# A hybrid RWKV-7 and DeltaNet block: lanes that take turns every 1280 dense columns, later norm sums, and a TensorE queue in emission order

## The chip, the cores and the metric

The kernel runs on one core of one Trainium2 chip. The metric is device time in microseconds (us). TensorE is PE in the views (its weight loads PEld), VectorE is DVE, ScalarE is ACT, GpSimd is POOL, and SP is the queue that issues nearly all transfers.

## The reference, cut to what matters

One layer over 256 latent and 256 context tokens of width 2048, in float32. An adaLN-modulated norm feeds one wide projection. Its columns go to an RWKV-7 branch (16 heads of 64, handled as 8 pairs), a gated DeltaNet branch (8 heads of 128) and merge gates:

```python
p = h @ in_w
pa, pb, pg = split_cols(p, [A_COLS, B_COLS, GATE_COLS])
ya, ya_c = rwkv7_branch(...)      # token shift, then two scans (forward and reverse) over the tokens
yb, yb_c = gdn_branch(...)        # conv, silu, l2 norm, then chunked scans
x = x + g1 * ((gate_a * (ya @ up_a) + gate_b * (yb @ up_b)) @ out_w)
x = x + g2 * squared_relu_mlp(modulate(rms_norm(x, norm2_w), sh2, sc2), mlp_w1, mlp_w2)
```

In the RWKV scan, `S_t = S diag(w) - (S kk) b^T + v k^T`; the kernel does it in chunks of 64 tokens, with the inverse of a triangular matrix per chunk. DeltaNet does likewise in chunks of 128.

## The kernel before, in words

Every large product is dense: weights are read in granules of 512 KB, split into a rounded part `hi` on ScalarE (L226) and a rest `lo` on VectorE (L227), and `mm3` (L239 to L241) issues three matmuls for each 128 rows of the contraction (a k-step), on 256 columns (latent tokens alone) or 512 (both). Results gather in two banks of PSUM (`dacc`, pool `psd`).

The middle of the kernel is the weave (L180). One generator, `dense`, goes through the projections of the layer and yields after each k-step with its cost, columns over 800. Beside it stand three lanes: `chains` (the recurrences: eight RWKV chains, then eight DeltaNet chains), `invs` (the triangular inversions) and `preps` (what an inversion and a chain need). After each dense yield, a lane whose due time has come emits one step or more; a step's cost is its yield times the lane's factor. A lane waits (`until`) for sets such as `ready`, `prepped`, `begun`, `done` and `read`, which are filled as the other generators are emitted; while `dense` itself is in an `until`, it yields 0.5 without a matmul.

A chain step is a group of small matmuls (L878, L896, L912 with L917 and L919) and the evictions of its result, on ScalarE or VectorE (L175 in the views, where a helper records them); the next step reads what was evicted. An inversion (`tri_inv`, L469) is 62 small operations on VectorE between transposes, after which L818, L828 and L841 use it on TensorE (L1153 on for DeltaNet). `prep2` emits L676, L678, L751, L748, L778 and L789 for each pair of heads. A norm sum (L611 for q and k, L654 for the RWKV key) is one matmul on squares that several evictions made. `gemv_steps` (L279) multiplies the modulation's weights (L296), one step per so many dense yields (`every`, MR).

The order of emission isn't the order of the queues. The tool that lays the queues out gives each engine the earliest emitted instruction that it takes to be ready, so a ready instruction can overtake one that isn't; `high_priority` (V1, S1, G1 and the casts) moves instructions ahead. SP's queue is laid out in the same way.

Of the kernel before, what the change touches and what calls it, by code (L numbers as in the profile page):

```python
# [20 lines left out]
NP = 8  # L21
# [5 lines left out]
CW, F_C, F_P, Q, GW, F_GP, GCW, F_GC, NG, MR, Y = 1.5, 1.5, 0.9, 0.0, 1.65, 0.9, 1.2, 0.6, 2, 16, (2, 2.5, 2, 2, 0, 1)  # L27
# [104 lines left out]
def body(tc, A, out, dbg=None):  # L132
# [146 lines left out]
    def gemv_steps(n, pool, acc, ahead=0):  # L279
# [3 lines left out]
        for q in range(4):  # L283
            raws = []
            for i in range(2):
                raw = pool.tile([128, 1024], F32, tag="raw", name="raw", bufs=ahead) if ahead else \
                    stream.tile([128, 1024], F32, tag="graw", name="graw", bufs=2)
                r0 = (4 * q + 2 * i) * 128
                nc.sync.dma_start(out=raw.rearrange("p (k c) -> p k c", k=2),
                                  in_=A["mod_w"][r0:r0 + 256, n * 512:(n + 1) * 512].rearrange("(k p) c -> p k c", p=128))  # L290
                raws.append(raw)
            if not ahead:
                yield
            for g in range(4):
                k = 4 * q + g
                P.matmul(out=pm[32 * g:32 * g + 32, :], lhsT=sc_st[:, 2 * k:2 * k + 32], rhs=raws[g // 2][:, g % 2 * 512:g % 2 * 512 + 512],  # L296
                         start=(q == 0), stop=(q == 3), skip_group_check=True)
            if q < 3:
                yield
        rows = (pool() if callable(pool) else pool).tile([128, 512], F32, tag="pt", name="rows", bufs=2)  # L300
        S.copy(out=rows, in_=pm)
        return rows, pm
# [103 lines left out]
    def projg(src, ncol, xonly):  # L406
# [3 lines left out]
        for g in range(2):  # L410
            wg = wgran(src[:, 8 * g:8 * g + 8, :])
            for kk in range(8):
                k = 8 * g + kk
                mm3(ps[:ncol, :n], *wk_(wg, kk, ncol), hT[k][0][:, tsl], hT[k][1][:, tsl], k == 0, k == KT - 1)
                yield n / 800
# [75 lines left out]
    def gate(j, tile_):  # L491

        ps = yield from projg(A["w_pg"][j], 128, True)
# [29 lines left out]
    with ExitStack() as st:  # L523
# [12 lines left out]
        def decays():  # L536
# [31 lines left out]
            V.tensor_scalar(out=bb, in0=bb, scalar1=0.5, scalar2=0.5, op0=ALU.mult, op1=ALU.add)  # L568
            for d in range(2):
# [12 lines left out]
                V.tensor_tensor(out=nbk, in0=nbk, in1=nb, op=ALU.mult)  # L582
                P.transpose(q[0:32, 128:256], gc, ident)
# [25 lines left out]
        def l2n(dst, n, bias, q, sq):  # L609
            S.activation(out=sq[:, :n], in_=dst[:, :n], func=AF.Square)  # L610
# [6 lines left out]
            V.tensor_tensor(out=dst[:, :n], in0=dst[:, :n], in1=sq[:, :n], op=ALU.mult)  # L617

        def gproj(h):
            ps = yield from projg(A["w_gdn"][h], 128, True)  # L620
            qv = ptile("qv")
            l2n(qv, 256, C("lnq"), ps, conv_silu(ps, qv, h, 256))
            nc.sync.dma_start(out=spq[h], in_=qv[:, :256])
            ps = yield from projg(A["w_gdn"][8 + h], 128, False)
            kv = ptile("kv")
            l2n(kv, 512, None, ps, conv_silu(ps, kv, 8 + h, 512))
            nc.sync.dma_start(out=spk[h], in_=kv)
            ps = yield from projg(A["w_gdn"][16 + h], 128, False)
# [9 lines left out]
        def prep(p, R):  # L638
# [6 lines left out]
            shifted((yield from psum(16, "v", False)), zv, 16 + p, 128, False)  # L645
            zr = rp.tile([128, SEQ], F32, tag="zr", name="zr", bufs=2)
            shifted((yield from psum(0, "r", True)), zr, p, 128, True)
            yield from until(lambda: p - 1 in prepped)
# [5 lines left out]
            P.matmul(out=ps, lhsT=C("b64"), rhs=t1, start=True, stop=True)  # L654
            S.activation(out=t1, in_=ps, func=AF.Ln, bias=C("eps_l2"))
            S.activation(out=t1, in_=t1, func=AF.Exp, scale=-0.5)
            kk = rp.tile([128, T], F32, tag="kk", name="kk")
            V.scalar_tensor_tensor(out=kk, in0=zk, scalar=W("kk", p), in1=t1, op0=ALU.mult, op1=ALU.mult)
            R.update(zk=zk, zv=zv, zr=zr, kk=kk)
            yield 0  # L660

        def prep2(p, R):
# [124 lines left out]
            V.scalar_tensor_tensor(out=bs, in0=bs, scalar=W("rk", p), in1=zr, op0=ALU.mult, op1=ALU.mult)  # L787
            q = pg()
# [5 lines left out]
        def inv2(p, R):  # L794
# [43 lines left out]
            for m in range(2):  # L838
                q = pr()
# [10 lines left out]
        def chain(p, R):  # L850
# [21 lines left out]
            for c in range(8):  # L872
# [27 lines left out]
                if c % 2 == 1 and c < 7:  # L900
                    yield CW / 2
# [3 lines left out]
                    yield CW / 2  # L905
                else:
                    yield CW
# [54 lines left out]
        for _ in prep(0, st_p[0]):  # L962
            pass
# [28 lines left out]
        def preps():  # L992
# [4 lines left out]
            decays()  # L997
# [13 lines left out]
        def work():  # L1011
            yield from rgates()
            for p in range(1, NP + 1):
                if p < NP:
                    yield from until(lambda: p - 2 in done)
                    yield from prep(p, st_p[p])
                    ready.add(p)
                yield from gproj(p - 1)
            for j in range(NG):
                yield from gate(j, lambda: ptile("gt"))  # L1020
# [242 lines left out]
        def upa(j):  # L1263
# [4 lines left out]
            for k in range(8):  # L1268
                mm3(ps[:, :256], *wk_(wg, k, 128), *uu[24 + k], k == 0, k == 7)
                yield 0.32  # L1270
# [63 lines left out]
        def works():  # L1334
            nonlocal every
            yield from work()
            every = 12
# [3 lines left out]
        weave(dense(lambda: every, works()),  # L1341
              [(both(chains(), stretch(F_GC / F_C, gchains())), F_C), (both(invs(), ginvs()), F_I),
               (both(preps(), stretch(F_GP / F_P, gpreps())), F_P)])
        for _ in md:
            pass
# [198 lines left out]
```

## Time and profile before

| | us |
|---|---|
| median of 3 runs | 2322.28 (2319.6 to 2328.75) |
| the profiled execution | 2330.75 |
| its span | 2329.0 |
| TensorE busy | 2220.3 |
| VectorE busy | 1581.7 |
| ScalarE busy | 1355.5 |

The profiled execution has a time of its own, 1.75 us above its span. Matmuls are pipelined, and the views give each from its start to its modelled end, so neighbours overlap; the distance between starts is what a matmul takes in a row.

### The profile page before, as it was taken

To read this page: it belongs to the slowest core of one execution; us is meant where nothing else is said; L and a number is where in the kernel's file an instruction comes from. 1 tells how busy PE (TensorE), PEld (TensorE's weight loads), DVE (VectorE), ACT (ScalarE), POOL (GpSimd) and SP (SyncE) were. 2 spreads that over 40 slices of the span, in tenths; PEclk is the share of its full clock that TensorE was granted. 3 is DMA by queue.
4 is the path that set the end of the run, shared out by engine and by line. 5 is a ranking of instruction groups with operands and counts; after the bars stand their busy time and mean duration, and the time that the engine had idled before them with its cause. 6 is when DMAs were issued, how large, how long until landed. Compare 5 with 4: busy or idle time off the path is not lost.

```text
span 2329.0 us, 45306 instructions
## 1 busy us (share of the span) xinstructions
PE 2220.3 (95%) x16886; PEld 1804.3 (77%) x16886; DVE 1581.7 (68%) x3590; ACT 1355.5 (58%) x3003; POOL 158.8 (7%) x343
## 2 busy tenths in 40 slices
PE   5989999999999999999999989999999999999997
PEld 2566676767677676788888888879999888999886
DVE  2366875868686867778577867876786555666555
ACT  3244758585867676765656766456455444555544
POOL 0000021111211121112000000000000000000000
PEclk9998999999999999999999989999999999999999
DMA  9953333433333333457575455875776666555664
GB/s 360 340 174 130 102 111 107 142 103 120 122 116 123 114 122 103 139 183 264 189 243 190 154 159 190 292 235 176 259 255 204 193 193 194 182 182 182 192 195 146
DMA packets 184660, 418.21 MB, mean 180 GB/s; under 512 B 15412, under 2 KB 37364, under 8 KB 183416
## 3 DMA queue, kind: packets, MB, share of 16 engines
q1 hardware_dynamic: 183864, 414.28, 54.6%
q8 instruction: 132, 2.16, 0.4%
q10 hardware_dynamic: 576, 1.05, 0.1%
q14 instruction: 88, 0.72, 0.1%
HBM read 399.76 MB, written 15.51 MB: 178 GB/s over the span
## 4 chain that ended last, share of the span: by engine, by line
PE 73%; ACT 8%; DVE 5%; DMA 4%; issue 2%; DVEq 0%; ACTq 0%; SPq 0%
PE dacc L239 14%; PE dacc L240 13%; PE dacc L241 12%; PE dacc L1430 3%; PE pm L1428 3%; PE pm L1429 3%; PE pm L1430 3%; PE dacc L1429 3%; PE dacc L1428 3%; DMA raw<-in_mod_w_dram 2%; PE vacc L296 2%; ACT hi L226 1%; DVE lo L227 1%; PE cb L878 1%; PE pg L748 1%
## 5 line engine op out<-in xcount | busy, mean ns | idle before, releaser
L226 ACT CAST hi<-raw 128x512 fp32r<-128x512 f32 (+1 forms) x1032 | 628.0, 610 | 639.6 <-PE dacc L240 341.1
L227 DVE TENSOR_TENSOR lo<-raw,hi 128x512 fp32r<-128x512 f32 (+1 forms) x1032 | 695.0, 677 | 446.1 <-ACT hi L226 258.4
L239 PE MATMUL dacc<-hh,hi 128*128 128x256 f32 (+1 forms) x1648 | 564.0, 342 | 14.6 <-DVE sg L444 5.8
L241 PE MATMUL dacc<-hh,lo 128*128 128x256 f32 (+1 forms) x1648 | 532.3, 323 | 0.6 <-DVE lo L227 0.6
L240 PE MATMUL dacc<-hl,hi 128*128 128x256 f32 (+1 forms) x1648 | 531.2, 322 | 0.6 <-DVE hl L245 0.6
L239 PEld LDWEIGHTS dacc<-hh,hi 128*128 128x128 f32 x1648 | 315.7, 192 | 82.9 <-issue 39.6
L241 PEld LDWEIGHTS dacc<-hh,lo 128*128 128x128 f32 x1648 | 316.5, 192 | 24.2 <-issue 2.6
L240 PEld LDWEIGHTS dacc<-hl,hi 128*128 128x128 f32 x1648 | 316.8, 192 | 21.1 <-issue 2.9
L241 PE MATMUL dacc<-ah,lo 128*128 128x258 f32 x1024 | 292.0, 285 | 4.6 <-DVE lo L227 4.4
L239 PE MATMUL dacc<-ah,hi 128*128 128x258 f32 x1024 | 291.3, 285 | 1.1 <-ACT ah L244 1.1
L240 PE MATMUL dacc<-al,hi 128*128 128x258 f32 x1024 | 290.8, 284 | 0.0
L241 PEld LDWEIGHTS dacc<-ah,lo 128*128 128x128 f32 x1024 | 194.9, 190 | 7.1 <-DVE lo L227 6.5
L239 PEld LDWEIGHTS dacc<-ah,hi 128*128 128x128 f32 x1024 | 195.0, 191 | 2.4 <-ACT ah L244 1.3
L240 PEld LDWEIGHTS dacc<-al,hi 128*128 128x128 f32 x1024 | 194.9, 190 | 1.1 <-issue 1.0
L175 POOL TENSOR_SCALAR sp<-vu,pc 64x64 f32<-64x64 f32 x224 | 128.3, 573 | 426.8 <-DVE vu L175 374.5
L1430 PE MATMUL dacc<-lo,hh 128*128 128x512 f32 x320 | 126.1, 394 | 4.5 <-DVE lo L227 4.5
L1428 PE MATMUL pm<-hi,hh 128*128 128x512 f32 x320 | 125.4, 392 | 0.0
L1429 PE MATMUL pm<-hi,hl 128*128 128x512 f32 x320 | 125.0, 391 | 0.0
L1430 PE MATMUL pm<-lo,hh 128*128 128x512 f32 x320 | 125.0, 391 | 0.0
L1428 PE MATMUL dacc<-hi,hh 128*128 128x512 f32 x320 | 124.9, 390 | 0.0
L1429 PE MATMUL dacc<-hi,hl 128*128 128x512 f32 x320 | 124.9, 390 | 0.0
L485 DVE TENSOR_TENSOR ltmp<-X,Lt 128x126 f32<-128x126 f32 (+22 forms) x372 | 93.9, 252 | 8.1 <-DMA X<-in_eye_dram 0.8
(414 smaller groups left out, 3239.0 us busy)
## 6 DMA issues: line engine op xcount, KB each, us to landing
raw<-in_w_dram SPq DMA_DIRECT2D x256, 512.0 KB
raw<-in_mod_w_dram SPq DMA_DIRECT2D x96, 512.0 KB
graw<-in_mod_w_dram SPq DMA_DIRECT2D x96, 512.0 KB
raw<-in_w_gdn_dram SPq DMA_DIRECT2D x64, 512.0 KB
raw<-in_w_pg_dram SPq DMA_DIRECT2D x64, 512.0 KB
raw<-in_w_rkv_dram SPq DMA_DIRECT2D x40, 512.0 KB
raw<-in_out_w_dram SPq DMA_DIRECT2D x32, 512.0 KB
raw<-in_upa_dram SPq DMA_DIRECT2D x16, 512.0 KB
```

Source lines behind the costliest of these rows:

```text
L175: return getattr(self.eng, name)(*a, **k)
L226: S.copy(out=hi[:, :F], in_=x)
L227: V.tensor_tensor(out=lo[:, :F], in0=x, in1=hi[:, :F].bitcast(F32), op=ALU.subtract)
L239: P.matmul(out=o, lhsT=wh, rhs=ah, start=first, stop=False)
L240: P.matmul(out=o, lhsT=wh, rhs=al, start=False, stop=False)
L241: P.matmul(out=o, lhsT=wl, rhs=ah, start=False, stop=last)
L296: P.matmul(out=pm[32 * g:32 * g + 32, :], lhsT=sc_st[:, 2 * k:2 * k + 32], rhs=raws[g // 2][:, g % 2 * 512:g % 2 * 512 + 512], start=(q == ...
L485: V.tensor_tensor(out=tv, in0=X[:, 0:n, j:j + 1].to_broadcast([128, n, 31 - j]), in1=Lt[:, j:j + 1, j + 1:32].to_broadcast([128, n, 31 - j ...
L748: P.matmul(out=q[:, c], lhsT=bkh(h, 4 + c), rhs=eb[r, h, c], start=True, stop=True)
L1428: P.matmul(out=pss[i], lhsT=ah[:, tsl], rhs=wh, start=first, stop=False)
L1429: P.matmul(out=pss[i], lhsT=al[:, tsl], rhs=wh, start=False, stop=False)
L1430: P.matmul(out=pss[i], lhsT=ah[:, tsl], rhs=wl, start=False, stop=last)
```

## The change

`turn` counts the dense columns and lets `projg` and `upa` yield only when 1280 of them (1024 in the last part of the weave) have gone by, with their sum as the cost. Norm sums are emitted from inside the next projection, after its eighth k-step (`half`), with the square moved ahead of it and the store behind it. Some added yields put matmuls that read an eviction into a later turn (`decays`, L789, the second half of L841). A chain step's yield CW goes from 1.5 to 1.0. `prep(1)` takes v first, then the x-gates, then r, then `gproj(0)`, then k, and the first merge gate comes before pair 2. The modulation's loads are issued one step earlier, its steps come every 6 (then 5) yields, and a turn stands between the copy of its rows and their use. The weave stands in a manual schedule of TensorE: its queue there has the order of emission.

```diff
--- before.py
+++ after.py
@@ -24,7 +24,7 @@
 RM, RD = 2, 6
 F_I = 0.7
 F_GI = 1.1
-CW, F_C, F_P, Q, GW, F_GP, GCW, F_GC, NG, MR, Y = 1.5, 1.5, 0.9, 0.0, 1.65, 0.9, 1.2, 0.6, 2, 16, (2, 2.5, 2, 2, 0, 1)
+CW, F_C, F_P, Q, GW, F_GP, GCW, F_GC, NG, MR, Y = 1.0, 1.5, 0.9, 0.0, 1.65, 0.9, 1.2, 0.6, 2, 6, (2, 2.5, 2, 2, 0, 1)
 EC = 0.5 * math.exp(-0.5)
 
 
@@ -280,7 +280,8 @@
 
 
         pm = acc()
-        for q in range(4):
+
+        def load(q):
             raws = []
             for i in range(2):
                 raw = pool.tile([128, 1024], F32, tag="raw", name="raw", bufs=ahead) if ahead else \
@@ -289,16 +290,26 @@
                 nc.sync.dma_start(out=raw.rearrange("p (k c) -> p k c", k=2),
                                   in_=A["mod_w"][r0:r0 + 256, n * 512:(n + 1) * 512].rearrange("(k p) c -> p k c", p=128))
                 raws.append(raw)
-            if not ahead:
-                yield
+            return raws
+
+        nxt = None
+        if not ahead:
+            nxt = load(0)
+            yield
+        for q in range(4):
+            raws = nxt or load(q)
             for g in range(4):
                 k = 4 * q + g
                 P.matmul(out=pm[32 * g:32 * g + 32, :], lhsT=sc_st[:, 2 * k:2 * k + 32], rhs=raws[g // 2][:, g % 2 * 512:g % 2 * 512 + 512],
                          start=(q == 0), stop=(q == 3), skip_group_check=True)
             if q < 3:
+                if not ahead:
+                    nxt = load(q + 1)
                 yield
         rows = (pool() if callable(pool) else pool).tile([128, 512], F32, tag="pt", name="rows", bufs=2)
         S.copy(out=rows, in_=pm)
+        if not ahead:
+            yield
         return rows, pm
 
     def mod_cols(n, pool, slot, acc, ahead=0):
@@ -403,7 +414,19 @@
         for _ in prev:
             pass
 
-    def projg(src, ncol, xonly):
+    stint, gone = 1280, 0
+
+    def turn(n):
+
+        nonlocal gone
+        gone += n
+        if gone < stint:
+            return 0
+        r, gone = gone, 0
+        return r
+
+    def projg(src, ncol, xonly, half=None):
+
         ps = psd.tile([128, 512], F32, tag="d", name="dacc")
         n = 256 if xonly else 512
         tsl = slice(T - n, T)
@@ -412,7 +435,11 @@
             for kk in range(8):
                 k = 8 * g + kk
                 mm3(ps[:ncol, :n], *wk_(wg, kk, ncol), hT[k][0][:, tsl], hT[k][1][:, tsl], k == 0, k == KT - 1)
-                yield n / 800
+                if k == 7 and half:
+                    half()
+                c = turn(n)
+                if c:
+                    yield c / 800
         return ps
 
     def drain(g):
@@ -488,9 +515,9 @@
         V.transpose(out=xt.rearrange("p u (a r) -> p a r u", r=2), in_=X.rearrange("p a (b c) -> p a b c", b=2))
         return X
 
-    def gate(j, tile_):
-
-        ps = yield from projg(A["w_pg"][j], 128, True)
+    def gate(j, tile_, half=None):
+
+        ps = yield from projg(A["w_pg"][j], 128, True, half)
         gt = tile_()
         S.activation(out=gt[:, :SEQ], in_=ps[:, :256], func=AF.Tanh, scale=0.5)
         nc.sync.dma_start(out=yspill[:, j, :], in_=gt[:, :SEQ])
@@ -566,6 +593,7 @@
             V.scalar_tensor_tensor(out=gg, in0=e1, scalar=-1.0, in1=al_.unsqueeze(1).to_broadcast([128, 4, 16]), op0=ALU.mult, op1=ALU.mult)
             S.activation(out=bb, in_=abt[:, :, 16:32], func=AF.Tanh, scale=0.5)
             V.tensor_scalar(out=bb, in0=bb, scalar1=0.5, scalar2=0.5, op0=ALU.mult, op1=ALU.add)
+            yield 3
             for d in range(2):
                 q = pg()
                 hs = slice(8 * d, 8 * d + 8)
@@ -580,6 +608,7 @@
                 V.tensor_tensor(out=nbk, in0=q[:, 32:64], in1=gc, op=ALU.subtract)
                 S.activation(out=nbk, in_=nbk, func=AF.Exp)
                 V.tensor_tensor(out=nbk, in0=nbk, in1=nb, op=ALU.mult)
+                yield 2
                 P.transpose(q[0:32, 128:256], gc, ident)
                 row = c2[0:32, 256 + 128 * d:384 + 128 * d]
                 S.copy(out=row, in_=q[0:32, 128:256])
@@ -606,8 +635,8 @@
             V.scalar_tensor_tensor(out=dst[:, :n], in0=th[:, :n], scalar=1.0, in1=dst[:, :n], op0=ALU.add, op1=ALU.mult)
             return th
 
-        def l2n(dst, n, bias, q, sq):
-            S.activation(out=sq[:, :n], in_=dst[:, :n], func=AF.Square)
+        def l2n(dst, n, bias, q, sq, then):
+
             P.matmul(out=q[:, :n], lhsT=C("ones"), rhs=sq[:, :n], start=True, stop=True)
             S.activation(out=sq[:, :n], in_=q[:, :n], func=AF.Ln, bias=C("eps_l2x4"))
             if bias is None:
@@ -615,17 +644,21 @@
             else:
                 S.activation(out=sq[:, :n], in_=sq[:, :n], func=AF.Exp, scale=-0.5, bias=bias)
             V.tensor_tensor(out=dst[:, :n], in0=dst[:, :n], in1=sq[:, :n], op=ALU.mult)
-
-        def gproj(h):
-            ps = yield from projg(A["w_gdn"][h], 128, True)
+            nc.sync.dma_start(out=then, in_=dst[:, :n])
+
+        def squares(ps, dst, col, n):
+            sq = conv_silu(ps, dst, col, n)
+            S.activation(out=sq[:, :n], in_=dst[:, :n], func=AF.Square)
+            return sq
+
+        def gproj(h, half):
+            ps = yield from projg(A["w_gdn"][h], 128, True, half)
             qv = ptile("qv")
-            l2n(qv, 256, C("lnq"), ps, conv_silu(ps, qv, h, 256))
-            nc.sync.dma_start(out=spq[h], in_=qv[:, :256])
-            ps = yield from projg(A["w_gdn"][8 + h], 128, False)
+            sq = squares(ps, qv, h, 256)
+            ps = yield from projg(A["w_gdn"][8 + h], 128, False, lambda q=ps, t=sq: l2n(qv, 256, C("lnq"), q, t, spq[h]))
             kv = ptile("kv")
-            l2n(kv, 512, None, ps, conv_silu(ps, kv, 8 + h, 512))
-            nc.sync.dma_start(out=spk[h], in_=kv)
-            ps = yield from projg(A["w_gdn"][16 + h], 128, False)
+            sq = squares(ps, kv, 8 + h, 512)
+            ps = yield from projg(A["w_gdn"][16 + h], 128, False, lambda q=ps, t=sq: l2n(kv, 512, None, q, t, spk[h]))
             vv = ptile("vv")
             conv_silu(ps, vv, 16 + h, 512)
             nc.sync.dma_start(out=spv[h], in_=vv)
@@ -635,7 +668,7 @@
             V.scalar_tensor_tensor(out=gz[:, :256], in0=gz[:, :256], scalar=1.0, in1=ps[:, :256], op0=ALU.add, op1=ALU.mult)
             nc.sync.dma_start(out=spz[h], in_=gz[:, :256])
 
-        def prep(p, R):
+        def prep(p, R, first=None, between=None):
             def psum(src, n, xonly):
                 if (n, p) in early:
                     return early[n, p]
@@ -643,21 +676,28 @@
 
             zv = rp.tile([128, T], F32, tag="zv", name="zv", bufs=2)
             shifted((yield from psum(16, "v", False)), zv, 16 + p, 128, False)
+            if first:
+                yield from first
             zr = rp.tile([128, SEQ], F32, tag="zr", name="zr", bufs=2)
             shifted((yield from psum(0, "r", True)), zr, p, 128, True)
+            if between:
+                yield from between
             yield from until(lambda: p - 1 in prepped)
             zk = rp.tile([128, T], F32, tag="zk", name="zk")
             ps = yield from psum(8, "k", False)
             shifted(ps, zk, 8 + p, 128, False)
             t1 = ptile("t1")
             S.activation(out=t1, in_=zk, func=AF.Square, scale=W("kk", p))
-            P.matmul(out=ps, lhsT=C("b64"), rhs=t1, start=True, stop=True)
-            S.activation(out=t1, in_=ps, func=AF.Ln, bias=C("eps_l2"))
-            S.activation(out=t1, in_=t1, func=AF.Exp, scale=-0.5)
-            kk = rp.tile([128, T], F32, tag="kk", name="kk")
-            V.scalar_tensor_tensor(out=kk, in0=zk, scalar=W("kk", p), in1=t1, op0=ALU.mult, op1=ALU.mult)
-            R.update(zk=zk, zv=zv, zr=zr, kk=kk)
-            yield 0
+
+            def norm():
+                P.matmul(out=ps, lhsT=C("b64"), rhs=t1, start=True, stop=True)
+                S.activation(out=t1, in_=ps, func=AF.Ln, bias=C("eps_l2"))
+                S.activation(out=t1, in_=t1, func=AF.Exp, scale=-0.5)
+                kk = rp.tile([128, T], F32, tag="kk", name="kk")
+                V.scalar_tensor_tensor(out=kk, in0=zk, scalar=W("kk", p), in1=t1, op0=ALU.mult, op1=ALU.mult)
+                R.update(zk=zk, zv=zv, zr=zr, kk=kk)
+                ready.add(p)
+            return norm
 
         def prep2(p, R):
             zk, zv, zr, kk = (R[n] for n in ("zk", "zv", "zr", "kk"))
@@ -785,6 +825,7 @@
                 yield 1.5
 
             V.scalar_tensor_tensor(out=bs, in0=bs, scalar=W("rk", p), in1=zr, op0=ALU.mult, op1=ALU.mult)
+            yield 1.5
             q = pg()
             P.matmul(out=q[:, :256], lhsT=C("b64"), rhs=bs, start=True, stop=True)
             V.tensor_tensor(out=bs, in0=q[:, :256], in1=zv[:, 256:], op=ALU.mult)
@@ -836,6 +877,8 @@
 
             vt = rp.tile([128, 8, 64], F32, tag="vt", name="vt")
             for m in range(2):
+                if m:
+                    yield Y[3]
                 q = pr()
                 for c in range(4):
                     P.transpose(q[0:64, c * 128:c * 128 + 128], R["zv"][:, (4 * m + c) * 64:(4 * m + c) * 64 + 64], ident)
@@ -898,13 +941,10 @@
                     for h in range(2):
                         S1.copy(out=vs_[d][hr[h], ns[d] % 2, 1, h, :], in_=cbs[d][hr[h], 64:128])
                 if c % 2 == 1 and c < 7:
-                    yield CW / 2
                     nvs = [vload(d, sgm + 1) for d in range(2)]
                     if c == 5:
                         loaded.add(p)
-                    yield CW / 2
-                else:
-                    yield CW
+                yield CW
                 for d in range(2):
                     n = ns[d]
                     if c < 7:
@@ -959,8 +999,7 @@
                 yield 0.5
 
         st_p = [{} for _ in range(NP)]
-        for _ in prep(0, st_p[0]):
-            pass
+        drain(prep(0, st_p[0]))()
         ph0.close()
         psg = ph1.enter_context(tc.tile_pool(name="psg", bufs=2, space=PSUM))
         psc = ph1.enter_context(tc.tile_pool(name="psc", bufs=2, space=PSUM))
@@ -994,7 +1033,7 @@
                 yield from until(lambda: p in ready and p - 2 in read and p - 1 in begun)
                 yield from prep2(p, st_p[p])
                 prepped.add(p)
-            decays()
+            yield from decays()
 
         def invs():
             for p in range(NP):
@@ -1009,14 +1048,15 @@
                 read.add(p)
 
         def work():
-            yield from rgates()
-            for p in range(1, NP + 1):
+            half = yield from prep(1, st_p[1], rgates(), gproj(0, None))
+            yield from gate(0, lambda: ptile("gt"), half)
+            for p in range(2, NP + 1):
+                half = None
                 if p < NP:
                     yield from until(lambda: p - 2 in done)
-                    yield from prep(p, st_p[p])
-                    ready.add(p)
-                yield from gproj(p - 1)
-            for j in range(NG):
+                    half = yield from prep(p, st_p[p])
+                yield from gproj(p - 1, half)
+            for j in range(1, NG):
                 yield from gate(j, lambda: ptile("gt"))
 
 
@@ -1267,7 +1307,9 @@
             ps = psum_d()
             for k in range(8):
                 mm3(ps[:, :256], *wk_(wg, k, 128), *uu[24 + k], k == 0, k == 7)
-                yield 0.32
+                c = turn(256)
+                if c:
+                    yield c / 800
             V.scalar_tensor_tensor(out=gt, in0=gt, scalar=1.0, in1=ps[:, :256], op0=ALU.add, op1=ALU.mult)
             split(*uu[8 + j], gt)
 
@@ -1333,16 +1375,18 @@
 
         def works():
             nonlocal every
+            nonlocal stint
             yield from work()
-            every = 12
+            every, stint = 5, 1024
             yield from gwork()
 
         mpool = gpp
-        weave(dense(lambda: every, works()),
-              [(both(chains(), stretch(F_GC / F_C, gchains())), F_C), (both(invs(), ginvs()), F_I),
-               (both(preps(), stretch(F_GP / F_P, gpreps())), F_P)])
-        for _ in md:
-            pass
+        with tc.manual_schedule(engines={mybir.EngineType.PE}):
+            weave(dense(lambda: every, works()),
+                  [(both(chains(), stretch(F_GC / F_C, gchains())), F_C), (both(invs(), ginvs()), F_I),
+                   (both(preps(), stretch(F_GP / F_P, gpreps())), F_P)])
+            for _ in md:
+                pass
     ph1.close()
```

## Rows read from the trace of the kernel before

**Rows 1.** The page: busy time of each engine, share of the span, and instructions.
```profile
PE 2220.3 (95%) x16886; PEld 1804.3 (77%) x16886; DVE 1581.7 (68%) x3590; ACT 1355.5 (58%) x3003; POOL 158.8 (7%) x343
```

**Rows 2.** Stretches: length, then busy us (instructions) by engine, granted clock, DMA share, GB/s.
```profile
150.00:240.00 90.00, 80.43 (x474) 59.63 (x474) 64.28 (x142) 47.97 (x96) 3.87 (x6) 0.87 0.40 134
240.00:1140.00 900.00, 869.84 (x7713) 645.40 (x7713) 658.48 (x1662) 605.57 (x1475) 146.76 (x316) 0.99 0.41 134
1140.00:1440.00 300.00, 279.80 (x2679) 252.03 (x2678) 219.16 (x640) 197.23 (x461) 6.80 (x10) 0.97 0.57 181
...
208.00:226.00 18.00, 17.14 (x85) 10.03 (x85) 9.54 (x21) 5.22 (x18) 0.23 (x2) 0.57 0.11 40
```

**Rows 3.** Timeline of TensorE at the start: start us, us, instructions [idle before].
```profile
164.99 0.55 PE L239 MATMUL dacc<-hh,hi 128*128 128x256 f32 x1 [5.82 <-DVE sg L444]
...
168.99 0.41 PE L240 MATMUL dacc<-hl,hi 128*128 128x256 f32 x1
169.20 0.41 PE L241 MATMUL dacc<-hh,lo 128*128 128x256 f32 x1
```

**Rows 4.** Timeline of TensorE: lane groups between dense matmuls.
```profile
605.70 0.39 PE L240 MATMUL dacc<-hl,hi 128*128 128x512 f32 x1
605.93 0.39 PE L241 MATMUL dacc<-hh,lo 128*128 128x512 f32 x1
606.25 0.45 PE L896 MATMUL cb<-rs,ti 64*64 64x64 f32 x8
...
606.97 0.39 PE L240 MATMUL dacc<-hl,hi 128*128 128x512 f32 x1
...
669.23 0.28 PE L240 MATMUL dacc<-hl,hi 128*128 128x256 f32 x1
669.35 0.28 PE L241 MATMUL dacc<-hh,lo 128*128 128x256 f32 x1
...
671.07 0.28 PE L240 MATMUL dacc<-hl,hi 128*128 128x256 f32 x1
```

**Rows 5.** Groups by line: count, busy us, mean ns, idle before and its releasers.
```profile
L485 DVE TENSOR_TENSOR ltmp<-X,Lt 128x126 f32<-128x126 f32 (+22 forms) x372 | 93.9, 252 | 8.1 <-DMA X<-in_eye_dram 0.8
```

**Rows 6.** Timeline of VectorE around one inversion.
```profile
303.65 2.00 DVE L476 STREAM_TRANSPOSE Lt<-dg 128x1024 f32<-128x1024 f32 x1
...
340.28 1.10 DVE L488 STREAM_TRANSPOSE ti<-X 128x512 f32<-128x512 f32 x1
```

**Rows 7.** Waits of TensorE, 240 to 1140 us: us in total, times, longest.
```profile
PE dacc L611 <- ACT gth L610: 7.0, 7, 2.0
PE pr L818 <- DVE ti L488: 3.0, 6, 0.9
...
PE cb L912 <- ACT vu L175: 2.5, 1, 2.5
PE pr L841 <- ACT ti L832: 2.1, 3, 1.6
PE pr L841 <- ACT vt L843: 1.9, 2, 1.7
```

**Rows 8.** Waits of TensorE, 150 to 240 us.
```profile
PE dacc L239 <- DVE sg L444: 5.8, 1, 5.8
PE pg L751 <- DVE bk L710: 2.5, 2, 1.6
```

**Rows 9.** Timeline of TensorE: the later part of prep2 of the first heads.
```profile
190.31 0.34 PE L778 MATMUL pg<-cs,bk 64*128 64x64 f32 x2
...
223.28 1.22 PE L789 MATMUL pg<-bs,cs 128*128 128x256 f32 x2
```

**Rows 10.** Groups by line: evictions on VectorE.
```profile
L175 DVE SCALAR_TENSOR_TENSOR vu<-cb,pc,sp 64x64 f32<-64x64 f32 x224 | 59.9, 282 | 24.0 <-PE cb L912 11.9 <-PE cb L919 6.9 <-POOL sp L175 0.9
...
L175 DVE SCALAR_TENSOR_TENSOR rs<-cb,gl,vt 128x128 f32<-128x128 f32 x48 | 15.9, 348 | 6.8 <-PE cb L1207 5.9
```

**Rows 11.** Waits of TensorE, 1140 to 1440 us.
```profile
PE cb L1216 <- DVE rs L175: 2.5, 4, 1.2
```

## The prediction

> **What bounds the kernel now.** I read the page first: TensorE (PE) is busy 95% of the span, no other engine over 68%, so time goes only where TensorE waits, runs at its lower clock, or changes between kinds of matmul [rows 1]. The stretches come next [rows 2]. The change touches the weave, about 150 to 1440 us. There TensorE is idle 9.6 us (150 to 240), 30.2 (240 to 1140, the RWKV chains) and 20.2 (1140 to 1440, the DeltaNet chains), 60 us in all. [...] After 1440 nothing is touched.
>
> The third cost is lone groups. Eight small chain matmuls between 512-column ones stretch 605.93 to 606.97, 1.04 us where two dense steps take 2 x 0.23; the group costs 0.58. Three such groups in a row (669.35 to 671.07, less two steps of 0.12) cost 1.48, or 0.49 each [rows 4]. Hence about 0.13 us for each change from dense to small and back that is saved.
>
> [...]
>
> **What the order of emission is.** I walked the weave by hand through its yields (columns over 800, due times, conditions), counted the dense matmuls emitted ahead of each lane matmul, and compared this with the order in the trace. Chain steps (64 of each kind) stand at the emitted place almost to the matmul, preparation steps after the first two heads mostly within ten. What is overtaken is what hangs on an inversion: L818 runs after 74 to 125 dense matmuls that are emitted behind it, for all eight heads, 19 to 40 us late, median 24; the second and third DeltaNet inversions run 26 and 38 us late, and their chains with them. The rows say why: one inversion is 62 small VectorE operations of 0.25 us [rows 5] and transposes of 2.0 and 1.1, 19 us alone; it begins at 303.65 and comes to its last transpose at 340.28, so half of VectorE's time goes to others meanwhile [rows 6]. L818 then still waits 0.5 us for it in the mean (3.0 in 6) [rows 7]. So manual order on TensorE changes nothing for most of the queue, and for the inversions it takes away the overtaking.
>
> **The change part by part**, against the profiled execution's own 2330.75 us.
>
> *Start.* Today the x-gates come first while v1 holds one of the two dense banks; TensorE waits 5.8 us for `sg`, then 2.5 for bk [rows 8]. With zv of v1 first and gproj(0) between r and k of prep(1), the second bank is free and 31 units of dense work cover preparation 0: -8. The stretches at low clock follow these waits [rows 3, 2]: -8 of 10. But the wait moves: prep(2) now reaches its k projection with preparation 1 not emitted; by my walk 28 groups of lane work (16 chain steps, the later part of prep2) stand in the queue with no dense matmul between. The same stretch of prep2 took 33 us beside dense work, 190.31 to 223.28 [rows 9]; alone it can't be under its matmuls, 8 us of chain groups (16 at 0.5) and about as much of prep2's and the modulation's. Idle of 4 to 25 (33 less the chain's 8); I take 9, nearer the low end because the two lanes fill each other's waits. The four gate groups L987 in a row share one `pr` bank: +2. Sum -5.
>
> *Coarser turns.* A turn comes after three 512-column steps (1536) or five of 256 (1280), 1.92 or 1.6 of the weave's units. A chain step is due every 1.0 x 1.5 = 1.5, so each turn takes exactly one, and what falls into one turn shares one change. My walk counts 447 groups emitted before and 336 after; the trace, where overtaking splits groups, shows 502. Between 111 and 166 changes at 0.13: -14 to -22; -21, since manual order ends the splitting.
>
> *Sums a turn later.* L611 waits 7.0 us for gth [rows 7]; its matmul now follows eight more k-steps, 2.9 us at 256 columns or 5.5 at 512, against a chain of conv, tanh and square whose waits today are 2.0 at most: -7. The added turns in inv2, at L789 and in decays take away most of L841's 4.0 [rows 7]: -3. Without the cover (an eviction over 5.5 us behind other work) the 7 stay.
>
> *Chain steps closer.* 2.25 units before, 1.6 to 1.92 now; in time 15 x 0.12 = 1.8 or 9 x 0.23 = 2.1 us. The longest eviction is four operations of 0.28 on VectorE [rows 10], 1.1 us and what VectorE is at just then; the others are shorter. It comes 56 times, so 0 to 25 us (0.45 each); I take +3, since the longest wait of today's is one of 2.5 [rows 7] and half of the turns hold other lanes' matmuls too.
>
> *Inversions.* Each inversion step (1.5 x 0.7 = 1.05) now takes a whole turn, so L818 is emitted 18 to 19 units after its preparation instead of 10 to 11, with 13 groups between instead of 7: 8 us of dense work and 6 x 0.58 later, 12 us. Of the lag of 24, 12 are left. While TensorE stands no new evictions come, and VectorE, half of which the inversion had, has it alone: 6. The other end is the 0.5 of today's wait. On eight heads and two DeltaNet inversions 0.5 to 12 each; I take 1.2, near the measured row, because waits of TensorE ahead of it give VectorE time as well: +12. Behind a standing L818 stand all dense matmuls, behind these the weight casts, and the chain of that head.
>
> *DeltaNet chains.* A step there is due every 1.2 x 0.6 = 0.72 and a turn is 1.28, so two steps often share one; my walk finds 36 such pairs, the second needing what ScalarE or VectorE evicts of the first (0.35 us [rows 10]) with nothing between. Where such a wait is seen today it is 0.6 (2.5 in 4, the longest 1.2) [rows 11]. 36 x 0.62 = 22, less the 2.5: +20; bounds 0 (evicted in time) and 36 x 1.2 = 43.
>
> *Queues.* The modulation's steps come each 6 (later 5) turns instead of 16 (12) yields, 72 in place of 96, and fit the some 75 offered. Its two loads are issued right behind the matmuls that free their buffers, so on SP the weight loads may stand behind them; three weight buffers ahead cover that (24 dense matmuls of half a 256-column projection take 2.9 us): 0, and without cover some 48 x 0.5 = 24. The stores of q and k move by half a projection; nobody reads them until the DeltaNet stage.
>
> Sum: -5 - 21 - 7 - 3 + 3 + 12 + 20 = -1, that is 2329.7 for a profiled execution. The profiled one stands 8.5 us above the median, 2322.28, so 2321 for the median: no change that can be told. Under 0.5%, 11.6 us either way, is about what a measurement of this kernel can't tell from none.
>
> [...]
>
> **Rivals.**
>
> *The evictions are in time* (faster, chance 0.32). The inversions wait 0.5 (-7), the pairs and chain steps nothing (-20, -3), the wait at prep(2) is 4 (-5). For it: chain steps stand at their emitted place today and hardly wait [rows 7]. Against: pairs have no dense work between. 2321 - 35 = 2286 us, 2262 to 2300.
>
> *TensorE stands at the inversions* (slower, 0.24). At 5 us on ten they cost 50, not 12; and a stand of 5.8 us was followed by 4.3 at the lower clock [rows 3], 1.9 lost each, 19. For it: the lag is there for all eight, and VectorE is full. Against: the turns bring 12 us. It decides from 3.5 us each. 2321 + 57 = 2378, without the clock 2359.
>
> *The clock* (slower, 0.06). [...]
>
> *Balance* (my forecast, 0.38): 2300 to 2340.
>
> **How the numbers follow.** Faster by over 0.5% is below 2310.7: the first rival and 0.11 of the forecast, 0.43. Slower is above 2333.9: 0.24 + 0.06 + 0.06 = 0.36. The rest is 0.21. The range 2266 to 2382 leaves out about 0.05 of the first rival's low end and 0.14 of the slow ones' high ends.
>
> **What would show it.** In the profile after: no wait for `sg`; L611 no longer waiting for gth; a stretch with no dense matmul ahead of prep(2)'s k, with 4 to 25 us of idle; L818 with its eight waits, 0.5 each or 5; L1207, L1216 and L1230 waiting about 0.6 some 36 times; a granted clock near 0.99 in the chains. I am wrong if L818's sum passes 30 us or if the idle of the weave falls below 40.

## The result, and the profile after

The changed kernel takes 2441.37 us (median of 4 runs, 2436.35 to 2447.25), the kernel before 2324.09 beside it: ratio 1.0499 [1.0476, 1.0522], 117 us slower. The profiled execution has a span of 2439.8 us, 111 above that of before.

The page of the changed kernel, and four stretches (the weave now ends near 1535):

```profile
PE 2211.7 (91%) x16886; PEld 1815.3 (74%) x16886; DVE 1594.7 (65%) x3590; ACT 1354.3 (56%) x3003; POOL 154.3 (6%) x343
```

```profile
150.00:240.00 90.00, 71.86 (x458) 54.83 (x456) 57.01 (x116) 47.07 (x93) 2.44 (x6) 0.87 0.39 131
240.00:1110.00 870.00, 762.51 (x6618) 565.24 (x6618) 603.74 (x1503) 539.93 (x1307) 128.08 (x288) 0.93 0.35 115
1110.00:1535.00 425.00, 374.38 (x3684) 335.49 (x3684) 282.86 (x790) 254.39 (x598) 22.47 (x38) 0.95 0.53 168
1535.00:2440.00 905.00, 878.03 (x5478) 791.75 (x5476) 596.23 (x1052) 466.43 (x918) 0.00 (x0) 0.99 0.63 208
```

TensorE's work is the same (16886 matmuls, 2211.7 us against 2220.3 [rows 1]). Its idle time in the weave went from 60 us [rows 2] to 18.1 + 107.5 + 50.6 = 176. These 116 us are as much as the whole loss; what the lower clock cost and what fewer changes saved (both below) nearly cancel. Sorted by length over the records of the weave, idle times over 3 us went from 1 (5.8 us in all) to 18 (81.0), those of 1 to 3 us from 18 (30.1) to 32 (54.9).

A stand, in what follows, is TensorE waiting idle at the head of its queue for an operand. Who is waited for, TensorE from 150 to 1535 us of the changed kernel (us in total, times, longest):

```profile
PE pr L859 <- DVE ti L515: 21.4, 5, 6.9
PE pg L818 <- DVE mb L805: 16.3, 13, 2.4
PE dacc L693 <- ACT t L690: 16.2, 6, 3.5
PE pr L1193 <- DVE xt L515: 13.2, 3, 6.4
PE pr L884 <- ACT vt L886: 12.4, 5, 3.9
PE cb L1256 <- DVE rs L175: 10.4, 12, 1.6
PE dacc L640 <- ACT gth L651: 9.5, 3, 5.2
PE pg L600 <- issue: 7.8, 1, 7.8
PE first_k L693 <- ACT t L690: 6.9, 1, 6.9
PE pr L1026 <- DVE sg L1016: 6.1, 2, 3.1
PE dacc L239 <- ACT hh L244: 5.5, 4, 2.5
...
PE pr L884 <- ACT y L984: 4.2, 2, 3.5
PE cb L1270 <- ACT vn L175: 4.1, 9, 1.4
PE cb L1281 <- DVE gs L175: 3.2, 8, 0.9
PE pr L859 <- DVE X L846: 3.1, 5, 1.2
PE cb L1270 <- DVE vn L175: 2.9, 3, 1.1
```

(Lines moved with the change: L859 is L818 of before, L818 is L778, L693 is L654, L640 is L611, L884 is L841, L1193 is L1153, L1256 is L1216, L1026 is L987, L600 is in `decays`.) The list is long and flat: inversions 37.7 us (21.4, 3.1, 13.2), norm sums 32.6 (L640, L693 twice), DeltaNet chain steps 20.6, `vt` 16.6, preparation 16.3. No single wait carries the loss. In the kernel before, two of these were short (150 to 1440 us):

```profile
PE pr L1153 <- DVE xt L488: 2.2, 2, 1.6
PE pg L778 <- DVE mb L765: 1.4, 2, 1.2
```

One stand in full, TensorE and then VectorE of the changed kernel:

```profile
487.25 0.28 PE L241 MATMUL dacc<-hh,lo 128*128 128x256 f32 x1
492.69 0.31 PE L859 MATMUL pr<-ti,off 32*32 32x32 f32 x2 [5.16 <-DVE ti L515]
```

```profile
486.49 0.21 DVE L514 TENSOR_TENSOR X<-X,ltmp 128x45 f32<-128x45 f32 x1
486.68 0.69 DVE L227 TENSOR_TENSOR lo<-raw,hi 128x512 fp32r<-128x512 f32 x1
487.29 0.41 DVE L175 TENSOR_TENSOR y<-y,cb 128x256 f32<-128x256 f32 x1
488.89 0.75 DVE L697 SCALAR_TENSOR_TENSOR kk<-zk,vs,t 128x512 f32<-128x512 f32 x1 [1.19 <-ACT t L695]
...
491.60 1.04 DVE L515 STREAM_TRANSPOSE ti<-X 128x512 f32<-128x512 f32 x1
```

TensorE reaches L859 while the inversion has four small operations and a transpose to go. VectorE does not have the inversion alone, as the prediction had it: it takes a weight rest, a chain's sum, the key and a convolution in between, and idles 1.19 us for ScalarE.

### The profile page after: what moved, and what is told of

The parts are those of the page before. It is cut to its first block, busy times and chain, and to the rows that moved or that the text cites. A ratio compares the mean times of both kernels' runs of the same rounds, so it can differ in the third digit from the quotient of the medians.

```text
span 2439.8 us, 45315 instructions
## 1 busy us (share of the span) xinstructions
PE 2211.7 (91%) x16886; PEld 1815.3 (74%) x16886; DVE 1594.7 (65%) x3590; ACT 1354.3 (56%) x3003; POOL 154.3 (6%) x343
## 4 chain that ended last, share of the span: by engine, by line
PE 40%; DVE 4%; DMA 3%; ACT 3%; issue 1%; SPq 0%; ACTq 0%; DVEq 0%
PE dacc L239 6%; PE dacc L240 6%; PE dacc L241 6%; PE dacc L1474 3%; PE pm L1473 3%; PE pm L1472 3%; PE pm L1474 3%; PE dacc L1473 3%; PE dacc L1472 3%; DMA raw<-in_mod_w_dram 2%; DVE lo L227 1%; ACT hi L226 1%; PE cb L1256 0%; PE cb L1281 0%; DMA yr<-ysp 0%
## 5 line engine op out<-in xcount | busy, mean ns | idle before, releaser
L239 PE MATMUL dacc<-hh,hi 128*128 128x256 f32 (+1 forms) x1648 | 583.1, 354 | 9.5 <-ACT hh L244 5.5
L239 PEld LDWEIGHTS dacc<-hh,hi 128*128 128x128 f32 x1648 | 326.7, 198 | 57.7 <-issue 20.5
L240 PEld LDWEIGHTS dacc<-hl,hi 128*128 128x128 f32 x1648 | 327.9, 199 | 25.4 <-issue 8.1
L241 PEld LDWEIGHTS dacc<-hh,lo 128*128 128x128 f32 x1648 | 326.7, 198 | 24.9 <-DVE lo L227 2.8
L239 PE MATMUL dacc<-ah,hi 128*128 128x258 f32 x1024 | 291.2, 285 | 1.1 <-ACT ah L244 1.1
L239 PEld LDWEIGHTS dacc<-ah,hi 128*128 128x128 f32 x1024 | 195.3, 191 | 2.4 <-ACT ah L244 1.3
```

The costliest lines, as they stand in the source:

```text
L239: P.matmul(out=o, lhsT=wh, rhs=ah, start=first, stop=False)
L240: P.matmul(out=o, lhsT=wh, rhs=al, start=False, stop=False)
L241: P.matmul(out=o, lhsT=wl, rhs=ah, start=False, stop=last)
```

## The experiments

Ratios are to the kernel before, timed beside each run. Three theories stood at the outset: A, TensorE, no longer able to overtake, stands where operands are late, with time at the lower clock behind it; B, the coarse turns cost; C, the late sums cost.

**Emission order taken out of the change, and put alone into the kernel before.**

```diff
-        with tc.manual_schedule(engines={mybir.EngineType.PE}):
+        if True:
             weave(...)
```

> The changed kernel with the manual schedule of TensorE taken away, all else kept. Theory A (the lost overtaking makes TensorE stand, and the clock falls behind it): most of the 117 us comes back, 2300 to 2345 us, the weave's idle of TensorE falls from 176 to 60 to 90 us. Theory B (coarse turns, with chain steps closer, make the waits themselves): 2400 or more, idle stays above 140. Theory C (the sums a turn later and the new order of the first projections make them): 2380 to 2420.

2324.78 us, 0.9994 [0.9975, 1.0012], and the idle time of the weave is 69 us, as theory A had it. Some of its waits:

```profile
PE dacc L640 <- ACT gth L651: 10.2, 7, 2.3
PE first_k L693 <- ACT t L690: 6.5, 1, 6.5
PE pr L859 <- DVE ti L515: 5.5, 7, 1.5
PE pg L818 <- DVE mb L805: 1.6, 3, 0.8
```

So the waits at L640 and for the first head's key norm (`first_k`), 16.4 of the 32.6 us of norm sums, stand without emission order too. The opposite edit, the `with` line around the weave of the kernel before and nothing else:

> The kernel before with TensorE's queue in the order of emission and nothing else changed. Theory A: the inversions, whose matmuls stood 24 us late behind overtaking work, now hold the queue 8 to 20 us each (ten of them), with a lower clock behind: 2430 to 2550 us. Theory B and theory C: 2315 to 2340, as nearly all other matmuls stand at their emitted place already.

2601.06 us, 1.118 [1.1149, 1.1211], above theory A's range, which had only the inversions. Its longest sums of waits:

```profile
PE dacc L611 <- ACT gth L610: 83.8, 16, 7.8
PE pr L818 <- DVE ti L488: 76.9, 7, 13.1
PE dacc L654 <- ACT t L653: 19.1, 4, 5.3
```

So emission order costs 275 us in the old order of emission and 117 in the new one; the rest of the change gives some 160 us back under emission order, and nothing where the tool lays the queue out. The norm sums of q and k alone (L611) stood 83.8 us: today they are overtaken, as the inversions are. In the trace of before, L611 runs 15 to 35 dense matmuls behind the place where emission order puts it, and the key norm (L654) 29 to 48.

**Coarse turns alone** in the kernel before (`stint` 1280, then 1024; CW 1.0; the modulation every 5, then 4 yields).

> The kernel before with coarse turns alone (1280, later 1024 columns; chain yields of 1.0; modulation steps every 5, later 4 turns), the tool's order, sums in place. Theory A: 2295 to 2335 us, with some 100 to 170 fewer changes between dense and small groups. Theory B: 2390 to 2440. Theory C: 2300 to 2335.

2323.11 us, 0.9978 [0.9954, 1.0002]. Neutral or nearly. Counting in the traces how often dense work is interrupted in the weave: 517 times before, 492 here and in the run without emission order, 334 in the changed kernel. The tool splits the groups again, so most of the fewer changes need the order that costs more.

**One wait taken away**: the inversion's first matmul later, `Y[2]` from 2 to 8.

> The changed kernel with one size changed: the yield ahead of L859 (L818 of before) goes from 2 to 8, so that it comes some three turns (8 us) later. Theory A with the inversions as the main stand: the 24.5 us of waits at L859 fall below 5 us, the clock rises, 2395 to 2425 us. If the inversion is only one of many stands (A with the sums, the banks and the DeltaNet pairs beside it): 2425 to 2440.

2404.31 us, 1.0347 [1.0329, 1.0365]: 37 us less, or 35 by the ratios. The 24.5 us of L859 left the list; the key norm's rose from 16.2 to 22.3. In all the weave's idle time fell by 17 us (176 to 159), and what dense matmuls lost at the lower clock by an estimated 10 to 13 (counted as in the part on the clock below); the granted clock from 240 to 1140 us went from 0.93 to 0.95.

**By stage.** The manual schedule left before the DeltaNet stage's dense work:

(Shortened: the `with` around the weave becomes `if True:`.)

```diff
+            cm.__enter__()
             yield from work()
+            cm.__exit__(None, None, None)
             every, stint = 5, 1024
```

> The changed kernel with TensorE in emission order only while the RWKV chains run; the planner orders the DeltaNet stage as before. Theory A (every place where TensorE reaches a matmul before its operand is there costs the wait and some time at the lower clock behind it, each stage by itself): idle of the changed kernel was 126 us up to 1110 and 51 behind it, against 40 and 20 before, so about three quarters of the 117 us are the RWKV stage's: 2400 to 2415. Rival P (the 36 pairs of DeltaNet chain steps without dense work between are the main cost): under 2375.

2401.46 us, 1.0325 [1.0293, 1.0357]: 79 us over before, the RWKV stage's part; the 40 that are missing to the changed kernel would be the DeltaNet stage's, by difference alone. The other half, entered there instead:

> The other half: emission order on TensorE only from the end of the RWKV stage's dense work on. Theory A: 2345 to 2365 (30 us more idle and the clock behind it). Rival P: over 2385. If this run and the one before it together give much more or less than 117 us over the kernel before, the stages do not stand each by itself (a lag that one stage passes on to the next).

2443.03 us, 1.0515 [1.0497, 1.0532]. This edit did not do what it was meant to: TensorE's queue came out the same as the changed kernel's through the whole weave. It is a repetition of that kernel, and says nothing on the stages; that the two add is not shown.

**Several stands at once.** `Y` to (2, 4, 8, 4, 0, 1), and the norm at `k == 14` instead of 7 (this moves all three sums, q's and k's as well as the key norm, since one `half` serves them):

> The changed kernel with three steps emitted later, all of them places where TensorE stood: the inversion's first matmul 8 units behind it instead of 2 (as in the run that gave 2404), preparation steps 4 instead of 2.5 units apart, the inversion's later steps 4 instead of 2, and the key norm six dense groups later. Theory A: the waits named for these (16 + 16 + 12 us in the changed kernel besides the inversion's 24) go for the most part, and the lower clock behind them: 2404 less 25 to 45, so 2360 to 2380. Rival M (in emission order a stand that is taken away comes back at the next matmul that is early, so the sum hardly moves): 2395 or more.

2400.13 us, 1.0332 [1.0309, 1.0354]. Theory A missed; it lies in rival M's range. Then DeltaNet steps a turn apart, `F_GC` from 0.6 to 1.1:

> The changed kernel with DeltaNet chain steps due every 1.2 x 1.1 = 1.32 units instead of 0.72, so that each takes a turn of its own. Theory A: the waits at the pairs were 10.4 (rs), 7.0 (vn) and 3.2 (gs) us in all, about half of them go and some are now hidden: 2425 to 2440. Rival P: 2400 or less. The prediction's own +20 for the pairs: about 2420.

2413.69 us, 1.0394 [1.0375, 1.0413]: 28 us less, 24 by the ratios, between the ranges of A and P and about what the prediction had for the pairs. It is more than the 10 us of waits that I had expected back: the waits at L1256 and L1270 went from 17.4 to 2.2, and the weave's idle time fell by 17. And both kinds with the later norm (`Y[2]` 8, `F_GC` 1.1, `k == 14`):

> The changed kernel, emission order kept, with only the three edits that attack single stands: the inversion's first matmul 8 units behind it (37 us in its own run), DeltaNet chain steps a turn apart (28 us in its own run), the key norm seven dense groups later (waits of 16 us). The preparation keeps its spacing. Theory A (stands are places by themselves and add): 2441 less 37, 28 and some 10 = 2355 to 2375. Rival M (what is taken from one stand comes back at the next): 2390 or more. Either way it stays above the kernel before, since the waits for mb, vt and gth are left (some 40 us).

2415.66 us, 1.0366 [1.0334, 1.0398]. Missed by 40. Its waits from 150 to 1600 us:

```profile
PE dacc L239 <- ACT gth L641: 19.4, 10, 4.9
PE pr L1193 <- DVE xt L515: 17.5, 3, 8.0
PE pg L818 <- DVE mb L805: 17.4, 12, 2.3
PE pg L788 <- DVE ea L808: 13.7, 8, 5.1
...
PE dacc L239 <- DVE vv L632: 7.4, 2, 5.0
```

The norm sum uses the bank of the projection it belongs to. Later by seven k-steps, it holds one of the two dense banks longer, and the next projection's first matmul (L239) stands instead: 19.4 us behind ScalarE's read of a sum (L641), and 7.4 more behind v's convolution (L632), where L640 and L693 had 25.7 in the changed kernel. Without that edit:

> As the run with three edits, which gave 2415.7, but without the later key norm, which held one of the two dense banks longer (TensorE waited 19 us for the next projection's bank behind gth and 7 behind vv there). Theory A' (stands add, and the later norm alone took back what was won): 2441 less 37 less 28, so 2370 to 2385. Rival M (any stand that is taken away comes back at the next): 2400 or more.

2398.74 us, 1.0316 [1.0277, 1.0355]: 43 us less, where the two edits by themselves gave 37 and 28. So the later norm won nothing; that it cost the 17 us between the two runs is not shown, for the two intervals overlap and the largest rise is at another place (L788 for `ea`, 13.7 us against 5.9). The time lies between the two theories: L859 is gone, but

```profile
PE dacc L693 <- ACT t L690: 22.6, 7, 4.7
PE pr L1193 <- DVE xt L515: 19.5, 3, 8.1
PE pg L818 <- DVE mb L805: 17.3, 14, 2.7
PE dacc L640 <- ACT gth L651: 12.7, 6, 3.6
```

rose by 6.4, 6.3, 1.0 and 3.2 against the changed kernel, 17 us, and that is most of the 22 that are missing. I read it so: a stand also gives VectorE and ScalarE time to catch up, and when it is taken away, the next early matmul stands longer. No run takes this apart.

**The start.** The old order of the dense work, emission order kept:

> The changed kernel with the old order of the dense work at the start (x-gates first, then all of preparation 1, then the first DeltaNet head), emission order kept. The prediction's term for the new order was -5, so 2446 by it. By the changed kernel's waits at the start (18 us idle between 150 and 245 against 10) and the 9 us idle in the stretch without dense work ahead of preparation 2's k: 15 less, 2421 to 2433, if the old order keeps its 10 under emission order.

2451.8 us, 1.0519 [1.0482, 1.0556]. My reading of the waits (15 less) fell. What the new order is worth can't be told: 10 us by the medians, 5 by the ratios, and the intervals of this run and of the changed kernel overlap.

**A version to keep.** The changed kernel without emission order and with DeltaNet steps a turn apart:

> The changed kernel without emission order, and with DeltaNet chain steps a turn apart. Theory A: where the planner may put dense matmuls between the two steps of a pair, pairs cost nothing, so 2317 to 2332 like the run without emission order alone (2325). If pairs cost in themselves, some 15 to 28 us less, under 2311: then this would be a version faster than both kernels.

2311.52 us, 0.993 [0.9903, 0.9957], 0.7% under the kernel before and under the run without emission order (0.9994 [0.9975, 1.0012]). Which part is it? The pace alone in the kernel before:

> The kernel before with one number changed: DeltaNet chain steps due every 1.32 units instead of 0.72. If the gain of the run at 2311.5 (0.7% under the kernel before) lies in this pace alone, the ratio is 0.990 to 0.996. If it needs the coarse turns or the late sums as well, 0.998 to 1.003.

2341.28 us, 1.0056 [1.0032, 1.0081], slower, and outside both ranges. Pace and coarse turns, sums in their old place:

> The kernel before with the coarse turns (0.998 by themselves) and DeltaNet chain steps due every 1.32 units, sums where they were, order by the planner. If turns and pace add without the late sums: 0.990 to 0.995. If the late sums and the new start were needed for it: 0.997 to 1.001.

2317.51 us, 0.9951 [0.9936, 0.9966]. The pace costs alone and pays within the change (0.9994 to 0.993). With the coarse turns it is 0.5% under the kernel before, but whether it adds to them (0.9978 [0.9954, 1.0002]), and whether late sums and the new start add to the two, can't be told: the intervals overlap. Nor is it settled where the 13 us to the run without emission order lie; by the records, some 5 are idle time and an estimated 4 are changes (461 against 492, at 0.13).

## Why the prediction was wrong

It said 2321, no change; 2441 lies outside its range. The step that failed is the comparison of orders: "Preparation steps after the first two heads mostly within ten", hence "manual order on TensorE changes nothing for most of the queue". Two faults lie in it. I compared only the lanes' matmuls; the norm sums are emitted in the dense generator and were not looked at, though in the old order they cost most under emission order (83.8). The measure that found the lag of L818 would have found theirs: 15 to 48 dense matmuls, where the change moves them by 24. And ten dense matmuls are 1.2 us at 0.12 each or 2.3 at 0.23: an order that agrees within ten leaves room for a stand of that length at each place, and L818 (`mb`) has thirteen, the longest 2.4. The sum also had no term for the lower clock behind new stands; that stood with a rival alone.

Term by term, in us against before; "came" is the difference of the waits shown here and in [rows 7, 8, 11], or what the last column names; changes and clock are estimates:

| term | predicted | came | |
|---|---|---|---|
| inversions | +12 | +32 | 37.7 against 3.0 and, for L1153, 2.2 |
| norm sums | -7 | +26 | 32.6 against 7.0; 16.4 of them also without emission order |
| preparation (`mb`) | 0 | +15 | 16.3 against 1.4 |
| `vt` | -3 | +13 | 16.6 against 4.0 |
| `decays` | 0 | +8 | L600 |
| DeltaNet pairs | +20 | +17 | 20.6 against 3.5 (L1216 and L1230); 24 to 28 by the run |
| chain steps | +3 | 0 | |
| changes | -21 | -24 | 517 to 334, at 0.13 |
| start | -5 | +8 | idle from 150 to 240 us, 18.1 against 9.6, less 6.9 in the norm sums; ahead of prep(2)'s k 9.3, less 3.0 in `mb` |
| clock | in the start | +20 to +30 | dense matmuls at a granted clock of 0.5, below |

The first five were put at +2 and came as +94; that is most of the 112 by which the forecast span fell short. All rows make 115 to 125, where the span grew by 111. The pairs and the changes were right (my walk's 336 groups came as 334 interruptions), and so was the wait ahead of prep(2)'s k: a stretch without dense matmuls from about 304 to 340 us, with 9.3 us of idle where I took 9. The rest of the start was not. The dense matmuls no longer wait for `sg`, but in the same place TensorE waits 6.9 us for the first head's key norm, where the wait for `sg` was 5.8, and the granted clock from 150 to 240 us stayed at 0.87:

```profile
165.65 2.07 PE L693 MATMUL first_k<-t,cs 128*128 128x512 f32 x2 [6.95 <-ACT t L690]
```

The -8 that the start has for the clock, of 10 us, was my estimate, and no run shows that the new order gives it: by the trace's record 23.9 of these 90 us had a granted clock of 0.5 before and 23.9 after, and the clock there was 0.96 in the change without emission order and also with the coarse turns alone, which keep the old start.

That the parts outside emission order net to nothing (2324.8 measured, 2321 forecast) is right for the total, not term by term: without emission order neither the pairs' waits nor most of the saved changes are there.

*Sums a turn later* failed at the key norm. Under emission order the eight k-steps took q's and k's sums from 83.8 us to 9.5, though not to 0, but the key norm's (without the first head's) only from 19.1 to 16.2. I set the cover (eight k-steps, 5.5 us at 512 columns) against today's waits of at most 2.0. Those are the waits of a matmul that is already overtaken until its operand is nearly there; the true chain is longer. In the key norm's, of which the prediction said nothing, VectorE takes six shifted additions with an inversion's operations and weight rests between them, then ScalarE the square.

*Inversions*: the lag of 24 us with 12 bought back was sound; the 12 that were left were put at 1.2 each "near the measured row", the same wait of an already overtaken matmul. L859 came to 24.5 on eight heads, 3.1 each (five stood, three did not), beside three of DeltaNet of 4.4. The rival "TensorE stands at the inversions" names the right mechanism, at 5 each, but only a third of the places. My own test for being wrong, L818's sum over 30, was not even met.

*The clock* was not the main cost, but it was one. The granted clock fell from 0.99 to 0.93 in the RWKV chains, where the prediction looked for 0.99. Around the stand above (stretches of the changed kernel):

```profile
470.00:480.00 10.00, 10.00 (x92) 7.32 (x91) 8.93 (x28) 3.80 (x11) 0.00 (x0) 1.00 0.17 54
487.50:492.70 5.20, 0.04 (x2) 0.01 (x1) 3.91 (x11) 2.67 (x6) 0.00 (x0) 0.98 0.31 101
492.70:497.00 4.30, 3.80 (x70) 3.12 (x71) 1.05 (x3) 2.29 (x5) 2.40 (x8) 0.50 0.01 4
497.00:502.00 5.00, 4.48 (x76) 3.19 (x76) 0.42 (x1) 1.57 (x4) 0.00 (x0) 0.77 0.08 9
```

Behind the stand the granted clock is 0.50 for some 7 us. Besides small matmuls nine dense ones run there, eight of them followed by the next after 0.43 us, where 512 columns otherwise take 0.23 [rows 4]:

```profile
495.52 0.63 PE L241 MATMUL dacc<-hh,lo 128*128 128x512 f32 x1
495.94 0.63 PE L239 MATMUL dacc<-hh,hi 128*128 128x512 f32 x1
496.37 0.63 PE L240 MATMUL dacc<-hl,hi 128*128 128x512 f32 x1
```

The record of the granted clock in the traces of both kernels holds two values, 0.5 and 1. By it 51 us of the weave were at 0.5 before and 191 after, of which 37 idle, 64 under other matmuls and 90 under dense ones. Dense matmuls that follow another there after 0.205 to 0.222 us (256 columns) or 0.415 to 0.44 (512) are 56 before and 225 after; what they take above 0.12 and 0.23 adds to 7 and 28 us. With the less regular ones at that level it is 12 and 43. So the clock cost dense work some 20 to 30 us (an estimate; what the others lost is not known). My theory for the first runs, a price at the lower clock behind each stand, holds to that extent: the nine above took 4.0 us in place of 2.1, so they lost the 1.9 that the rival had for a stand (there 4.3 us of matmuls 0.21 apart [rows 3] instead of 0.12 [rows 4]).

Whether the laid-out queue overtakes is 2324.8 against 2441.4 us. With the queue in emission order no other matmul ran in the 5.16 us ahead of L859 above, and the next dense one came behind it, at 494.50; in the kernel before with emission order all sixteen L611 waited, 83.8 us in all.

## What to carry to other kernels

A short wait in a trace whose order has been chosen for readiness is no measure of how early the operand is: the matmul was put where the operand came. Before an order is fixed by hand, measure each operand's delay from the emission of its producer, for every kind of matmul (those in the dense stream too), and compare it with the work emitted between. Retime in the emission first, with the planner still laying out the queue; here the coarse turns with slower DeltaNet steps, without and with the rest of the change, gave 0.5 to 0.7% that way, and fixing the order took 5%. And when a stand is moved, look at which bank it now holds.

## What the runs showed of the hardware

During a stand of 5.2 us the granted clock stayed at 0.98; it was 0.50 in the 4.3 us behind it and 0.77 in the next 5, though the engine was working again. At 0.50 a dense matmul of 512 columns followed the last after 0.43 us instead of 0.23. The mean granted clock (0.984 to 0.956 over the span) does not tell the price by itself: of 191 us at 0.5 in the weave 101 were idle or under other matmuls, and the 90 under dense work cost some 20 to 30.
